# Weight matrices as contiguous chunks, cached keys transposed by the host, and two smaller moves, in a two-layer diffusion trunk

## The chip, the cores and the metric

The kernel runs on one core of a Trainium2 chip. Its metric is the device time of one execution in microseconds (us). Engines are named as in the profile: PE (TensorE), DVE (VectorE), ACT (ScalarE), POOL (GpSimd) and SP (SyncE, which issues most loads). DMA engines move data between HBM and SBUF, the on-chip memory of 128 partitions; PE writes to PSUM, from which ACT and DVE read.

## What is computed

One step of a trunk of two layers, on 128 context tokens and 256 latent tokens, 384 rows of width 2048, all in float32. Each layer modulates its normalized input, projects it, mixes tokens by attention, multiplies by a gate and projects back:

```python
m = silu(cond) @ ada_w + ada_b                       # 2048 -> 3 * 2048, for context and latent
shift, scale, gate = split(m, 3)
h = rmsnorm(x, norm_w) * (1 + scale) + shift
# layer one: 8 heads of differential attention beside a pooling mixer
q, k, v, u, g = split(h @ even_w_in, ...)            # 2048 -> 6144
x = x + gate * ((concat(attn, pool) * silu(g)) @ even_w_out)
# layer two: grouped-query attention, 16 query heads, 4 key heads of 128
q, k, v, g = split(h @ gqa_w_in, ...)                # 2048 -> 5120
x = x + gate * ((attn * silu(g)) @ gqa_w_out)
```

Queries and keys are normalized per head and rotated (latent tokens only). Latent tokens attend to 128 cached context keys as well (`cache_a_k` of layer one, 8 heads of 128 by 128; `cache_c_k` of layer two, 4 heads). Outputs are x of both groups and the new context keys and values.

## The kernel before

All work is traced by the class `Trunk` into a list of items, and `run` goes through it: each item is loaded eight items ahead (`load`), split four items ahead (`split_w`) and then executed. A planner with a model of each instruction's time puts the traced instructions of every engine in order and gives out the buffers; the order in which the code traces them is their priority.

A weight item (`"w"`) is a chunk of 512 KB: two blocks of 128 rows (k blocks) by 512 columns for the token projections (`tok_proj`), or four by 256 for the gates (`gate_proj`); the first chunks of layer one and a few of layer two are single k blocks of 256 KB. `load` fetches it by one DMA on SP's queue into one of two `raw` tiles (L402). `split_w` casts it on ACT into a high part `wh` (L451) and subtracts on DVE for a low part `wl` (L452), three buffers each. Each product is three matmuls of high and low parts (`mm3`, L476 to L478): 128 by 128 by 512 columns for token projections, by 384 for gates. `ada_w` is fetched in loads of 256 KB into `aw` (seven) or `acc` (four) tiles: items `"ada"` go to PE (L413, L544), in groups of one or two blocks of 128 columns at the start (`GROUPS`), items `"adav"` to DVE (L420, L610). A load's row in HBM is a piece of a row of the matrix: 512 bytes for the groups of one block, 1 KB for those of two, 2 KB for 512 columns.

The span begins with X: 12 loads of 256 KB, 48 transposes on PE (L263) whose results ACT copies out (L272), then the modulation in the order of `GROUPS`, each group followed by the chunks of the query and key projections that its rows allow.

Beside the items run generators (`side`, `urgent`), stepped once or twice per weight item: `qk_gen` normalizes, rotates and transposes (L718) a block of 512 query or key columns; `diff_gen` (layer one) and `gqa_gen` (layer two) are the heads; `cache_k` loads four cached heads at a time on POOL's queue into a `kq` tile (L741), transposes them on PE (L745) and, for layer one, ACT copies them into the key tiles `kT` (L752); for layer two they are split into high and low part (`hilo`, L773 and L774).

In layer two `qk_collect` copies the three token tiles of a block of 512 columns out of PSUM into `kq` tiles (L1085; six buffers, which also serve squares, rotation, gates and rows of the modulation), where they stay until L718 has transposed them. `b2` is a pool of 23 tiles of the same size: in layer two it holds the high and low keys and values (16 tiles), the context keys and values (2), the rotary rows, and the transposed probabilities of the heads (L926, L773). `g_finish` takes a gate bank out of PSUM by a tanh on ACT into a `kq` tile (L968) and a product on DVE (L969); the banks are four `mm` tiles, two per pair of gate blocks.

At the end of layer one the output projection runs in four blocks of 512 columns, each over eight chunks and three token tiles. For the last block `HOLD` is 2: `tok_proj` holds the chunk before the last and then runs both of them tile by tile. So the last 36 matmuls are 12 of tile 0, then 12 of tile 1, then 12 of tile 2. When a tile is complete, `out_finish` multiplies by the gate (L1025), adds (L1026), squares (L253), takes the root (L295 to L304) and makes two k blocks of the next h (L325 to L331) for that tile. Then layer two's key and value projections begin, whose first single chunks are split beforehand into `b2` tiles (L442, L443).

Of the kernel before, what the change touches and what calls it, by code (L numbers as in the profile page):

```python
# [17 lines left out]
P = 128  # L18
D = 2048
KT = D // P  # L20
# [31 lines left out]
HOLD = 2  # L52
BAND = 128 + 136 + 136


class Trunk:
# [338 lines left out]
    def load(self, it):  # L395
        nc = self.nc
        if it[0] == "w":
            _, w, kk, c0, nw, _ = it
            nk = len(kk)
            raw = self.p_raw.tile([P, nk, nw], F32, tag="raw", name=f"raw{self.uid()}")  # L400
            src = w[kk[0] * P:(kk[0] + nk) * P, c0:c0 + nw].rearrange("(k p) n -> p k n", p=P)
            self.last_load = nc.sync.dma_start(out=raw, in_=src).ins  # L402
            return raw
        if it[0] == "ada":
# [3 lines left out]
            for kk in range(k0, k0 + self.ada_span(nw), nk):  # L408
# [3 lines left out]
                src = self.io["ada_w"][l, kk * P:(kk + nk) * P, c0:c0 + nw].rearrange("(k p) n -> p k n", p=P)  # L412
                nc.sync.dma_start(out=raw, in_=src)  # L413
                raws += [raw[:, i, :] for i in range(nk)]
            return raws
        if it[0] == "adav":
            _, l, k, c0, nw, _ = it
            nk = 512 // nw
            raw = self.t_aw().rearrange("p (k n) -> p k n", k=nk)
            nc.sync.dma_start(out=raw, in_=self.io["ada_w"][l, k * P:(k + nk) * P, c0:c0 + nw].rearrange(  # L420
                "(k p) n -> p k n", p=P))
            return raw
# [7 lines left out]
        return None  # L430

# [48 lines left out]
    def tok_proj(self, w, c0s, ks, act, finish, hold=1, single=0):  # L480
        banks = {}
        held = []

        def on_chunk(wt, kk, bi):
# [3 lines left out]
            held.append((wt, kk))  # L488
            if kk[0] in ks[-2 * hold:-2]:
                return  # L490
            for t in range(3):
                for (wh, wl), kh in held:
                    for i, k in enumerate(kh):
                        h = act[k]
                        a = (h[:, 0, t * P:(t + 1) * P], h[:, 1, t * P:(t + 1) * P])
                        self.mm3(banks[bi, t], a, (wh[:, i, :], wl[:, i, :]), k == ks[0], k == ks[-1])
                if kk[-1] == ks[-1]:
                    finish(bi, t, banks.pop((bi, t)))
            held.clear()
# [478 lines left out]
    def out_proj(self, l, w, ks, finish):  # L978
# [84 lines left out]
    def build(self):  # L1063
# [9 lines left out]
        W0 = io["even_w_in"][0]  # L1073
        W0o = io["even_w_out"][0]
        W1 = self.w1 = io["gqa_w_in"][0]
        W1o = io["gqa_w_out"][0]
# [68 lines left out]
        main.append(self.call(lambda: self.add_side(self.cache_k(io["cache_a_k"], 8))))  # L1145
# [65 lines left out]
        main.append(self.call(lambda: self.add_side(self.cache_k(io["cache_c_k"], 4, 1))))  # L1211
# [53 lines left out]

_INS = ["x_prompt", "x_sample", "cache_a_k", "cache_a_v", "cache_c_k", "cache_c_v", "c", "c_ctx", "norm_w", "ada_w",
# [24 lines left out]
```

## Time and profile before

| | us |
|---|---|
| median of 3 runs | 1240.4 (1239.6 to 1242.59) |
| the profiled execution | 1239.09 |
| its span | 1237.3 |
| PE busy | 1213.1 (98%) |
| DVE busy | 948.7 (77%) |
| ACT busy | 527.6 (43%) |
| POOL busy | 144.3 (12%) |
| granted TensorE clock, mean | 0.994 |

The span runs from the first to the last instruction; the profiled execution's own time holds a little more than its span. A busy PE is one with a matmul in its pipeline, whose ends are modelled, so neighbouring matmuls overlap in the rows. A timeline row gives start, length, engine, line, operation, tiles written and read, shape and count, and in brackets how long the engine was idle before it and what released it. A granted clock of 1.00 is 2.4 GHz, 0.50 is 1.2 GHz.

### The profile page before, as it was taken

The numbers are of one execution on the slowest core, as the hardware profiler recorded it, in microseconds if no ns is written. First come the engines' busy times: TensorE is split into PE (matmuls) and PEld (weight loads), VectorE is DVE, ScalarE is ACT, GpSimd is POOL, SyncE is SP. The second block draws the span as 40 slices with busy tenths as digits, with TensorE's granted clock in tenths as the row PEclk, the third lists the DMA queues.
The fourth block names the chain that finished last, engine by engine and source line by source line (L and its number), as shares of the span: only waits on it lengthen the run. The fifth ranks groups of instructions, "written<-read, shape, count | busy, mean of one in ns | idle before, by whom it ended". The sixth has DMA issues, their size and how long they took to land.

```text
span 1237.3 us, 18300 instructions
## 1 busy us (share of the span) xinstructions
PE 1213.1 (98%) x6519; PEld 1008.9 (82%) x6519; DVE 948.7 (77%) x1677; ACT 527.6 (43%) x1058; POOL 144.3 (12%) x172
## 2 busy tenths in 40 slices
PE   5999999999999999999999999999999999999998
PEld 4567678777879889997878678888889899998886
DVE  3678569799999799898894699978956985665343
ACT  4323234334445544563334454434544444553221
POOL 0000008611001101001000000423213000000000
PEclk9999999999999999999999999999999999999999
DMA  9999964887777466678785677754633433247652
GB/s 282 331 309 314 338 207 142 258 258 228 253 243 244 136 201 202 184 229 289 236 271 177 198 244 248 226 150 148 191 102 103 148 117 103 86 122 235 188 162 94
DMA packets 174781, 253.50 MB, mean 205 GB/s; under 512 B 14841, under 2 KB 86946, under 8 KB 174690
## 3 DMA queue, kind: packets, MB, share of 16 engines
q1 hardware_dynamic: 169506, 243.57, 62.7%
q0 software_dynamic: 3152, 5.56, 1.4%
q10 hardware_dynamic: 2032, 3.21, 0.7%
q8 instruction: 51, 0.84, 0.3%
q14 instruction: 40, 0.33, 0.1%
HBM read 244.39 MB, written 7.90 MB: 204 GB/s over the span
## 4 chain that ended last, share of the span: by engine, by line
PE 89%; DMA 5%; DVE 3%; ACT 1%; issue 1%; SPq 1%; POOL 0%; DVEq 0%; ACTq 0%; POOLq 0%
PE mm L476 25%; PE mm L477 24%; PE mm L478 24%; PE ax L544 3%; PE ax L476 2%; PE ax L477 2%; PE ax L855 1%; PE ax L478 1%; DVE acc L610 1%; DMA acc<-ada_w 1%; PE ax L875 1%; DMA raw<-even_w_in 1%; PE ax L959 1%; PE ax L924 1%; DMA raw<-even_w_out 1%
## 5 line engine op out<-in xcount | busy, mean ns | idle before, releaser
L451 ACT CAST wh<-raw 128x1024 fp32r<-128x1024 f32 (+1 forms) x242 | 250.8, 1037 | 453.3 <-PE mm L477 160.6
L452 DVE TENSOR_TENSOR wl<-raw,wh 128x1024 fp32r<-128x1024 f32 (+1 forms) x242 | 292.8, 1210 | 172.6 <-ACT wh L451 170.2
L476 PE MATMUL mm<-wh,h 128*128 128x512 f32 x1016 | 400.7, 398 | 2.6 <-ACT h L328 1.2
L477 PE MATMUL mm<-wh,h 128*128 128x512 f32 x1016 | 400.0, 394 | 0.0
L478 PE MATMUL mm<-wl,h 128*128 128x512 f32 x1016 | 392.5, 395 | 0.4 <-DVE wl L452 0.3
L610 DVE SCALAR_TENSOR_TENSOR acc<-aw,sT,acc 128x512 f32<-128x512 f32 x420 | 297.8, 745 | 0.0
L476 PEld LDWEIGHTS mm<-wh,h 128*128 128x128 f32 x1016 | 191.1, 188 | 52.4 <-issue 7.3
L478 PEld LDWEIGHTS mm<-wl,h 128*128 128x128 f32 x1016 | 191.4, 189 | 45.3 <-issue 3.9
L477 PEld LDWEIGHTS mm<-wh,h 128*128 128x128 f32 x1016 | 191.6, 189 | 40.3 <-issue 2.4
L476 PE MATMUL mm<-h,wh 128*128 128x384 f32 x512 | 175.6, 343 | 0.0
L477 PE MATMUL mm<-h,wl 128*128 128x384 f32 x512 | 174.6, 341 | 0.0
L478 PE MATMUL mm<-h,wh 128*128 128x384 f32 x512 | 173.8, 339 | 0.0
L476 PEld LDWEIGHTS mm<-h,wh 128*128 128x128 f32 x512 | 96.6, 189 | 2.6 <-issue 1.8
L477 PEld LDWEIGHTS mm<-h,wl 128*128 128x128 f32 x512 | 96.6, 189 | 2.3 <-issue 1.6
L478 PEld LDWEIGHTS mm<-h,wh 128*128 128x128 f32 x512 | 96.5, 189 | 0.6
L1105 DVE TENSOR_TENSOR b<-mm,b 128x512 f32<-128x512 f32 x72 | 47.8, 684 | 22.6 <-PE mm L478 22.4
L161 POOL TENSOR_TENSOR ss<-ss,mhalf 128x12 f32<-128x12 f32 (+1 forms) x9 | 31.5, 3503 | 263.1 <-DVE ss L159 263.1
L161 POOL TENSOR_TENSOR ti<-ti,mhalf 128x3 f32<-128x3 f32 (+1 forms) x12 | 15.5, 1293 | 211.8 <-DVE ti L159 211.8
L639 POOL DMA_DIRECT2D gates<-kq x32 | 15.7, 495 | 204.2 <-ACT kq L651 141.3
L544 PE MATMUL ax<-aw,sT 128*32 128x256 f32 (+2 forms) x412 | 38.3, 403 | 0.4 <-DMA aw<-ada_w 0.4
L807 ACT ACTIVATE p<-ax,ti 128x384 f32<-128x384 f32 (+1 forms) x48 | 24.2, 508 | 27.1 <-DVE ti L805 26.9
L702 POOL TENSOR_TENSOR kq<-kq,b 128x128 f32<-128x128 f32 x40 | 33.3, 867 | 9.3 <-DVE kq L691 5.9
(208 smaller groups left out, 1240.9 us busy)
## 6 DMA issues: line engine op xcount, KB each, us to landing
aw<-ada_w SPq DMA_DIRECT2D x333, 256.0 KB, 4.0
raw<-even_w_in SPq DMA_DIRECT2D x92, 512.0 KB, 4.6
raw<-gqa_w_in SPq DMA_DIRECT2D x78, 512.0 KB, 3.7
raw<-even_w_out SPq DMA_DIRECT2D x32, 512.0 KB, 4.6
raw<-gqa_w_out SPq DMA_DIRECT2D x32, 512.0 KB, 4.0
acc<-ada_w SPq DMA_DIRECT2D x51, 256.0 KB, 5.9
b<-x_sample SPq DMA_DIRECT2D x16, 256.0 KB, 5.4
kq<-gates SPq DMA_DIRECT2D x16, 256.0 KB, 4.7
```

Source lines behind the costliest of these rows:

```text
L161: nc.gpsimd.tensor_tensor(out=r, in0=t, in1=self.mhalf[:, :n], op=ALU.pow)
L451: nc.scalar.copy(out=wh, in_=raw)
L452: nc.vector.tensor_tensor(out=wl, in0=raw, in1=wh.bitcast(F32), op=ALU.subtract)
L476: mm(out, lhsT=a[0], rhs=b[0], start=start, stop=False, skip_group_check=skip)
L477: mm(out, lhsT=a[1], rhs=b[0], start=False, stop=False, skip_group_check=skip)
L478: mm(out, lhsT=a[0], rhs=b[1], start=False, stop=stop, skip_group_check=skip)
L544: mm = nc.tensor.matmul(b[q:q + 32, half * nw:half * nw + nw], lhsT=self.cond_cols(k0 + i), rhs=raw[i], start=k0 == 0 and i >= span - 4, s ...
L610: nc.vector.scalar_tensor_tensor(out=acc[c], in0=raw[:, i, :], scalar=s, in1=acc[c], op0=ALU.mult, op1=ALU.add)
L639: nc.gpsimd.dma_start(out=self.gates[l, c:c + 1, j * 512 + 256 * i:j * 512 + 256 * i + 256], in_=row[q:q + 1, 0:256])
L702: nc.gpsimd.tensor_tensor(out=t2g[:, :, qq * qd:(qq + 1) * qd], in0=q[:, :, pr * qd:(pr + 1) * qd], in1=sb.broadcast_to([P, G, qd]), op=AL ...
L807: nc.scalar.activation(out=e[:, :n], in_=s, func=AF.Exp, bias=mx[:, i:i + 1], accum_out=sm[:, i:i + 1])
L1105: nc.vector.tensor_tensor(out=r, in0=bank, in1=r, op=ALU.add)
```

## The change

The host cuts `ada_w` and the four large weight matrices into the tiles in which the kernel loads them, and stores each tile as 128 contiguous lines, one per partition: 4 KB a line for the weights (`_tiles`), 2 KB for `ada_w` (`_ada_tiles`). The class `Tiles` finds a chunk in them. Number, order, size and queue of the loads are the same; a chunk of a single k block is half of each line of its tile.

The cached keys come transposed from the host. In layer one each head's keys are loaded straight into the cached columns of its key tile, eight loads of 64 KB on POOL's queue; in layer two they are loaded into a `kq` tile as before and split from there. The transposes and, for layer one, the copies are gone.

The hold at the end of layer one is gone: the last block runs its chunks one by one like the others. And in layer two the three query rows of block 3 are copied into `b2` tiles instead of `kq` tiles.

```diff
+class Tiles:
+    def __init__(self, ap, gates):
+        self.ap, self.gates = ap, gates
+
+    def chunk(self, k, nk, c0, nw):
+        if c0 < self.gates:
+            tile_no = c0 // 512 * 8 + k // 2
+        else:
+            tile_no = self.gates // 512 * 8 + (c0 - self.gates) // 256 * 4 + k // 4
+        t = self.ap[tile_no].rearrange("p (k n) -> p k n", n=nw)
+        return t[:, k % (1024 // nw):k % (1024 // nw) + nk]
...
-            src = w[kk[0] * P:(kk[0] + nk) * P, c0:c0 + nw].rearrange("(k p) n -> p k n", p=P)
+            src = w.chunk(kk[0], nk, c0, nw)
...
-                src = self.io["ada_w"][l, kk * P:(kk + nk) * P, c0:c0 + nw].rearrange("(k p) n -> p k n", p=P)
-                nc.sync.dma_start(out=raw, in_=src)
+                nc.sync.dma_start(out=raw, in_=self.ada_tile(l, c0, kk // nk, nk))
...
+    def ada_tile(self, l, c0, j, nk):
+        return self.io["ada_w"][l * 12 * KT + c0 // P * 4 + j].rearrange("p (k n) -> p k n", k=nk)
...
-            held.append((wt, kk))
-            if kk[0] in ks[-2 * hold:-2]:
-                return
+            wh, wl = wt
             for t in range(3):
-                for (wh, wl), kh in held:
-                    for i, k in enumerate(kh):
...
+            if l == 0:
+                for h in range(b, b + 4):
+                    nc.gpsimd.dma_start(out=self.kT[h][:, P:2 * P], in_=src[h])
+                yield
+                continue
             ck = self.t_kq()
-            nc.gpsimd.dma_start(out=ck.rearrange("p (h d) -> p h d", h=4),
-                                in_=src[0, 0, b:b + 4].rearrange("h t d -> t h d"))
-            pt = self.t_aux()
-            for h in range(4):
-                nc.tensor.transpose(out=pt[:, h * P:(h + 1) * P], in_=ck[:, h * P:(h + 1) * P], identity=self.ident)
+            nc.gpsimd.dma_start(out=ck.rearrange("p (h t) -> p h t", h=4),
+                                in_=src[b:b + 4].rearrange("h d t -> d h t"))
             for h in range(4):
-                src_ = pt[:, h * P:(h + 1) * P]
-                if l:
-                    self.hilo(self.kH[h][:, 0:P], self.kL[h][:, 0:P], src_)
-                    self.kready.add(h)
-                else:
-                    self.evac(1, "c", self.kT[b + h][:, P:2 * P], src_)
+                self.hilo(self.kH[h][:, 0:P], self.kL[h][:, 0:P], ck[:, h * P:(h + 1) * P])
+                self.kready.add(h)
...
-            blk = self.tok_proj(w, [n * 512], ks, yT, lambda bi, t, bank, n=n: finish(n, t, bank),
-                                HOLD if l == 0 and n == 3 else 1)
+            blk = self.tok_proj(w, [n * 512], ks, yT, lambda bi, t, bank, n=n: finish(n, t, bank))
...
-                r = self.t_kq()
+                r = self.t_b2() if l == 1 and blk0 + bi == 3 and not which else self.t_kq()
...
+def _cut(w, nk, nw):
+    n = w.shape[1] // nw
+    return w.reshape(KT // nk, nk, P, n, nw).transpose(3, 0, 2, 1, 4).reshape(-1, P, nk * nw)
+
+
+def _tiles(w, gates):
+    return np.ascontiguousarray(np.concatenate([_cut(w[:, :gates], 2, 512), _cut(w[:, gates:], 4, 256)]))
```

## Rows read from the trace of the kernel before

**Rows 1.** The page: span, busy time of each engine (share of the span) and instructions.

```profile
span 1237.3 us, 18300 instructions
...
PE 1213.1 (98%) x6519; PEld 1008.9 (82%) x6519; DVE 948.7 (77%) x1677; ACT 527.6 (43%) x1058; POOL 144.3 (12%) x172
```

**Rows 2.** The waits of PE, whole span: us in total, times, longest us.

```profile
PE ax L203 <- DMA p<-norm_w: 5.7, 1, 5.7
...
PE ax L476 <- ACT r L773: 2.8, 2, 2.4
PE ax L544 <- DMA acc<-ada_w: 1.8, 3, 1.1
...
PE ax L544 <- DMA aw<-ada_w: 0.4, 1, 0.4
```

**Rows 3.** The table of stretches: busy us of each engine, granted clock, DMA share, GB/s.

```profile
10.00:12.00 2.00, 2.00 (x12) 2.00 (x11) 1.26 (x4) 1.82 (x6) 0.00 (x0) 1.00 1.00 368
15.00:19.00 4.00, 3.80 (x43) 2.97 (x42) 1.01 (x5) 3.43 (x10) 0.88 (x1) 1.00 1.21 297
26.00:32.00 6.00, 5.97 (x27) 4.12 (x28) 1.05 (x3) 0.96 (x2) 0.00 (x0) 0.50 1.15 322
26.00:170.00 144.00, 143.18 (x952) 96.99 (x953) 94.78 (x196) 45.29 (x72) 0.00 (x0) 0.98 0.98 320
694.00:698.00 4.00, 4.00 (x12) 3.13 (x11) 1.23 (x5) 0.56 (x2) 1.33 (x2) 0.57 0.29 95
967.00:971.00 4.00, 3.15 (x12) 3.15 (x13) 4.00 (x9) 1.55 (x5) 0.45 (x1) 0.57 0.73 228
```

**Rows 4.** Timeline of PE, start of the span: start us, us, instruction, idle time before.

```profile
9.19 8.31 PE L263 MATMUL ax<-ident,b 128*128 128x128 f32 x48
...
21.86 0.42 PE L544 MATMUL ax<-acc,sT 128*32 128x128 f32 x8 [1.14 <-DMA acc<-ada_w]
...
26.03 2.07 PE L476 MATMUL mm<-wh,h 128*128 128x512 f32 x4 [1.03 <-ACT h L328]
...
58.03 0.64 PE L544 MATMUL ax<-acc,sT 128*32 128x256 f32 x8 [0.42 <-DMA acc<-ada_w]
```

**Rows 5.** Instructions of single lines: ns min/median/max, first and last start.

```profile
L745 PE MATMUL ax<-ident,kq x12: 272/273/330, 261.1 to 791.3; 128*128 128x128 f32 x12
...
L741 POOL DMA_DIRECT2D kq<-cache_a_k x2: 752/788/825, 249.1 to 250.0; - x2
...
L759 POOL DMA_DIRECT2D b<-cache_a_v x8: 534/542/624, 206.3 to 229.3; - x8
```

**Rows 6.** Timelines of ACT and PE, layer two, block 3 and the first gates.

```profile
920.08 0.58 ACT L1089 COPY kq<-mm 128x512 f32<-128x512 f32 x1
...
964.22 1.01 PE L718 MATMUL ax<-ident,kq 128*128 128x128 f32 x6
...
965.13 0.89 ACT L968 ACTIVATE kq<-mm 128x384 f32<-128x384 f32 x2
...
967.86 0.58 PE L476 MATMUL ax<-r,r 128*128 128x256 f32 x1 [2.38 <-ACT r L773]
...
969.16 0.67 PE L476 MATMUL mm<-h,wh 128*128 128x384 f32 x1
```

**Rows 7.** Timeline of all engines, end of layer one.

```profile
685.01 0.69 DVE L1025 TENSOR_TENSOR kq<-mm,kq 128x512 f32<-128x512 f32 x1 [0.53 <-PE mm L478]
...
686.74 0.69 DVE L443 TENSOR_TENSOR r<-raw,r 128x512 fp32r<-128x512 f32 x1 [1.03 <-ACT r L442]
...
687.34 0.68 DVE L1026 TENSOR_TENSOR b<-b,kq 128x512 f32<-128x512 f32 x1
...
689.57 0.39 PE L476 MATMUL mm<-wh,h 128*128 128x512 f32 x1
...
689.80 0.39 PE L477 MATMUL mm<-wh,h 128*128 128x512 f32 x1
...
692.52 0.47 PE L476 MATMUL mm<-r,h 128*128 128x512 f32 x1
```

More of the change, by code (lines that the diff above doesn't have):

```diff
@@ L51 @@
 EARLY_H = 2
-HOLD = 2
 BAND = 128 + 136 + 136
+class Tiles:
[8 more added lines that the diff above has]
+        return t[:, k % (1024 // nw):k % (1024 // nw) + nk]
 class Trunk:
@@ L419, in load @@
             raw = self.t_aw().rearrange("p (k n) -> p k n", k=nk)
-            nc.sync.dma_start(out=raw, in_=self.io["ada_w"][l, k * P:(k + nk) * P, c0:c0 + nw].rearrange(
-                "(k p) n -> p k n", p=P))
+            nc.sync.dma_start(out=raw, in_=self.ada_tile(l, c0, k // nk, nk))
             return raw
@@ L478, in mm3, with tok_proj @@
         mm(out, lhsT=a[0], rhs=b[1], start=False, stop=stop, skip_group_check=skip)
-    def tok_proj(self, w, c0s, ks, act, finish, hold=1, single=0):
+    def tok_proj(self, w, c0s, ks, act, finish, single=0):
         banks = {}
-        held = []
         def on_chunk(wt, kk, bi):
@@ L487, in on_chunk @@
                     banks[bi, t] = self.t_mm() if bi * 3 + t < 4 else self.t_aux()
-            held.append((wt, kk))
-            if kk[0] in ks[-2 * hold:-2]:
-                return
+            wh, wl = wt
             for t in range(3):
-                for (wh, wl), kh in held:
-                    for i, k in enumerate(kh):
-                        h = act[k]
-                        a = (h[:, 0, t * P:(t + 1) * P], h[:, 1, t * P:(t + 1) * P])
-                        self.mm3(banks[bi, t], a, (wh[:, i, :], wl[:, i, :]), k == ks[0], k == ks[-1])
+                for i, k in enumerate(kk):
+                    h = act[k]
+                    a = (h[:, 0, t * P:(t + 1) * P], h[:, 1, t * P:(t + 1) * P])
+                    self.mm3(banks[bi, t], a, (wh[:, i, :], wl[:, i, :]), k == ks[0], k == ks[-1])
                 if kk[-1] == ks[-1]:
                     finish(bi, t, banks.pop((bi, t)))
-            held.clear()
         return self.w_items(w, c0s, ks, on_chunk, single)
@@ L1071, in build @@
             self.x_transpose(n)
[L1073 to L1076, printed above, removed]
+        W0 = Tiles(io["even_w_in"], 4096)
+        W0o = Tiles(io["even_w_out"], 2048)
+        W1 = self.w1 = Tiles(io["gqa_w_in"], 3072)
+        W1o = Tiles(io["gqa_w_out"], 2048)
         nat = list(range(KT))
@@ L1144, in build @@
         main = []
-        main.append(self.call(lambda: self.add_side(self.cache_k(io["cache_a_k"], 8))))
+        main.append(self.call(lambda: self.add_side(self.cache_k(io["cache_a_kt"], 8))))
         main.append(self.call(lambda: self.new_v(io["cache_a_v"], range(4))))
@@ L1210, in build @@
                 main.append(self.call(lambda: self.rope_tables(1)))
-        main.append(self.call(lambda: self.add_side(self.cache_k(io["cache_c_k"], 4, 1))))
+        main.append(self.call(lambda: self.add_side(self.cache_k(io["cache_c_kt"], 4, 1))))
         for b in range(4):
@@ L1263, in _tables, with _ada_tiles @@
     return {"k_cos_a": ca, "k_sin_a": sa, "k_cos_c": cc, "k_sin_c": sc, "k_band": bands, "k_sel": sel}
+def _cut(w, nk, nw):
[3 more added lines that the diff above has]
+    return np.ascontiguousarray(np.concatenate([_cut(w[:, :gates], 2, 512), _cut(w[:, gates:], 4, 256)]))
+def _ada_tiles(ada_w):
+    tiles = [_cut(ada_w[0, :, part * D + k0 * P:part * D + (k0 + nt) * P], 4 // nt, nt * P)
+             for part in range(2) for k0, nt in GROUPS]
+    tiles += [_cut(ada_w[0, :, 2 * D:], 1, 512), _cut(ada_w[1], 1, 512)]
+    return np.ascontiguousarray(np.concatenate(tiles))
 _INS = ["x_prompt", "x_sample", "cache_a_k", "cache_a_v", "cache_c_k", "cache_c_v", "c", "c_ctx", "norm_w", "ada_w",
@@ L1282 @@
     arrays.update(_tables())
+    arrays["ada_w"] = _ada_tiles(arrays["ada_w"])
+    for name, gates in (("even_w_in", 4096), ("even_w_out", D), ("gqa_w_in", 3072), ("gqa_w_out", D)):
+        arrays[name] = _tiles(arrays[name][0], gates)
+    for name in ("cache_a_k", "cache_c_k"):
+        arrays[name + "t"] = np.ascontiguousarray(arrays.pop(name)[0, 0].transpose(0, 2, 1))
     for name, a in arrays.items():
```

## The prediction, made before the changed kernel ran

> **What bounds the kernel now.** I read the page first [rows 1]: TensorE (PE) is busy 98% of a span of 1237.3 us, so only two things can move the time much: instructions taken off PE, and the 24 us in which PE stands still or runs at the lower clock. The chain of waits is of little use here, since it is nearly all PE. The second view is what PE itself waited for [rows 2]. The list is short: 5.7 us for one row of vectors at the start, 2.8 us for ACT work of layer two, and only 1.8 + 0.4 us for the `ada_w` loads. No wait of PE on a weight load of `even_w_in`, `gqa_w_in` or the output weights appears in that list at all. The third view is the table of stretches [rows 3]. From 26 to 170 us the DMA engines are busy 98% of the time at 320 GB/s, and yet PE is busy 143.18 of 144 us: in that stretch, the one with the most loading, transfers are hidden. The same table shows three places where the granted clock is down: 26 to 32 us (0.50), 694 to 698 (0.57) and 967 to 971 (0.57). All three stand at or right behind a gap of PE; 0.50 is 1.2 GHz of 2.4.
>
> So a better layout of the weights can pay only at the very start, where PE waits for loads with nothing else to do. The other parts of the change touch two of the gaps directly. I make the sum against the profiled execution, which took 1239.1 us (span 1237.3); the median of the runs is 1240.4, so 1.3 us are added at the end. A change under 0.3% (3.7 us) can't be told from none by the measurement.
>
> **Part A, contiguous weights.** Of each chunk the bytes stay the same and the pieces get longer: a first `ada_w` load (four k blocks by 128 columns) goes from 512-byte rows to 2 KB per partition, those of the pairs from 1 KB to 2 KB, a token chunk from two rows of 2 KB to one of 4 KB. The number of loads, their order on SP's queue and their buffers stay. At the start, X is loaded in 2 KB rows and the first loads of `ada_w` come behind it. PE is on the transposes of X from 9.19 to 17.5 us whatever the loads do, then on the eight loads of the first modulation group, the last of which it waits for at 21.86 us, and the first large matmul starts at 26.03 [rows 4]. In the stretch with the 2 KB rows the DMA engines moved 368 GB/s at a share of 1.00, in that with the 512-byte rows 297 GB/s, with a share that reads over 1 [rows 3]. Eight loads of 262,144 bytes are 2.10 MB: 7.1 us at 297 GB/s, 5.7 us at 368. The last lands about 1.4 us sooner, and the first large matmul moves with it, since all between is one chain through ACT and VectorE. The later waits for loads of `ada_w` (0.42 us at 58.03 [rows 4] and about 0.4 more in the sum of [rows 2]) go as well: 2.2 us in all, which is just what PE waited for these loads. The Trainium skill ("DMA: Bandwidth & Descriptors", Specifications) sets the smallest transfer for full rate at 512 bytes; by that page the old rows were long enough and part A would give nothing (+2.2 us on the sum). Here the rows differ, 297 against 368 GB/s [rows 3], and I go by them. Bounds: 0, if the chain from the last load has other limits; and a gain of 5.2, if the whole of the 2.2 goes and the 6 us at clock 0.50 behind it [rows 3], which cost 3.0, go too. For all other loads I count nothing: the work that hides them is PE's own, and without that cover (PE waiting for each landing) they would gain by about a tenth of the transfer. SP's queue gets shorter, never longer.
>
> **Part B, cached keys.** Twelve transposes leave PE [rows 5]. One takes 0.27 us, but they overlap: six transposes of the same shape (L718) take 1.01 us [rows 6], so they start (1.01 - 0.27) / 5 = 0.15 us apart. PE is spared 12 x 0.15 = 1.8 us, and all of this counts because PE is the bound. Eight ACT evacuations of layer one go too; in layer two the split into high and low part stays, read from the loaded tile in place of PSUM. In exchange GpSimd issues eight loads of 64 KB, straight into the key tiles, where there were two of 256 KB: by the 0.54 us of the `cache_a_v` loads, of the same size, 4.3 us in place of 1.6 [rows 5]. Behind them on that queue stand a row of `ada_b` and the four stores of `out_av`, which nothing of PE waits for soon. Between the old loads' issue at 249.1 and the first transpose that read them at 261.1 lie 12 us [rows 5], and the score matmuls come later still, so 2.7 us more are covered. If the cover were gone, PE would wait for at most these 2.7 us. Value: -1.8, bounds -1.8 and +0.9.
>
> **Part C, raw rows.** In layer two the three query rows of block 3 move from the `kq` tiles (six buffers) to the `b2` tiles (23). In the trace of before the last of them is written at 920.08 and the last transposes that read them run at 964.22 [rows 6]: half of the `kq` buffers are tied up for 44 us, while the gate projections run and need one `kq` per bank. And the first gate activations (L968) come only at 965.13, two at once, right behind those transposes and in front of the conversion (L773) that PE waits for 2.38 us; the next gate matmul starts at 969.16 with the clock down [rows 2, 6]. I read it so: all four banks of `mm` are full, no tile is there to empty them, and when one comes free ACT has it all to do at once. With the rows in `b2` the activations can run when their banks are complete. That takes away the 2.38 us, and up to 1.7 us of the stretch at clock 0.57 (4 us with 43% missing) [rows 3]. Together 4.1; I take 3.4, since ACT then still has the same work and the waits may leave a rest. What it costs: of the 23 `b2` tiles the keys, values and rotary rows of layer two hold 19, so the transposed probabilities of the heads (three per head) get one tile where they had four, as long as block 3's rows wait. No row of before shows a wait for `b2`. Nearest row: the 2.38 us that the shortage of `kq` cost. Bounds: -4.1, and the price in the second rival below.
>
> **Part D, the end of layer one.** Before, the last two chunks of the last output block are held back and run token tile by token tile, so tile 0 is complete two tiles of 12 matmuls ahead of the end; after, only the last chunk is, and tile 0 is complete 12 matmuls later than now. Matmuls start 0.23 us apart [rows 7], so that is 2.8 us. The work per tile (gate product, sum, squares, root, scaling, two tiles of h) is one chain of VectorE, ACT, GpSimd and PE. Before it began at 685.01 and the first matmul of layer two started at 692.52 [rows 7]. But in it the sum (L1026) stood from 685.70 to 687.34 behind a weight split (L443) on VectorE, and 2.8 us later that split is long done: 1.6 us come back. On the other hand the three tiles' chains lie closer: tile 1's gate product (0.68 us) falls into tile 0's chain, so I add 0.6. Sum: +2.8 - 1.6 + 0.6 = +1.8. Bounds: 0 (VectorE's order so that tile 0 goes through), and 2.8 + 1.7 = 4.5, if nothing comes back and a second stretch at the lower clock like 694 to 698 follows the longer gap [rows 3].
>
> **Sum.** A -2.2, B -1.8, C -3.4, D +1.8: -5.6 us, 1233.5 in the profiled execution and 1234.8 as median, 0.5% faster. The program is also put in order anew by the planner; I have no row for what that does, and it is inside the widths.
>
> **The rivals.**
> 1. Part C gives nothing, because VectorE and ACT in that stretch are the limit and not the tile: 1234.8 + 3.4 = 1238.2. For it: ACT was busy for all of 967 to 971 [rows 3]. Against it: that the first gate activations wait until the transposes are through.
> 2. Slower: the shortage moves from `kq` to `b2`. Two heads, six tiles, go through one buffer while block 3's rows wait. If a turn costs PE as much as the shortage of `kq` did, 2.4 us, the change is no longer measurably faster from two turns on (+4.8 against -5.6) and is measurably slower from four on; with all six it gives 1234.8 + 14.3 = 1249.1. Against it: gate matmuls fill PE in that stretch.
> 3. The change doesn't do at the start what it says, since the length of the rows doesn't set the rate: the start is as it was, 1234.8 + 2.2 = 1237.0. This is what the page's 512 bytes would come to. Against it: the two rates in [rows 3].
> 4. More than forecast: the shorter gap at the start spares the stretch at half clock (3.0 us) and part D costs nothing (1.8): 1234.8 - 4.8 = 1230.0.
>
> **How the numbers follow.** My forecast has 0.52, rival 1 0.16, rival 2 0.11, rival 3 0.10, rival 4 0.11. The forecast's own range is 1232 to 1238, by the bounds of C and D; its centre lies 1.9 us under the line of 1236.7, so 0.42 of its 0.52 are faster and 0.10 the same. Rival 1 is the same, rival 3 is divided (0.04 faster, 0.06 same), rival 4 is faster, and rival 2 is slower by 0.09 of its 0.11, the rest the same. Faster 0.57, same 0.34, slower 0.09. For 8 in 10 the range goes from 1229.5 (rival 4 inside) to 1242.0, and leaves out most of rival 2.
>
> **What would show it.** A: the first large matmul at about 24.6 us in place of 26.03, and no wait of PE for `ada_w`. B: no transposes at the old line, the first score matmuls not waiting for a DMA. C: gate activations spread between 935 and 965, no gap at 965, full clock there; wrong, if PE or ACT then waits in 920 to 960 for the tiles of the probabilities. D: the first matmul of layer two 1 to 3 us later against the last of layer one; wrong, if the gap is as before. The whole is wrong if PE shows new gaps in 170 to 690 us, where I expect none.

## The result: 1227.95 us, twice the forecast gain

The changed kernel takes 1227.95 us as the median of four runs (1227.69 to 1230.22), the kernel before 1241.3 us beside it on the same chip: a ratio of 0.9896, interval [0.988, 0.9911], or 13.35 us less. I had forecast 1234.8 us, 5.6 us less than before, with a range from 1229.5 to 1242.0. The sign was right, the size was not, and the range was too high at its lower end. Two later comparisons of the same kernel give 0.9903 [0.9886, 0.9921] and 0.9913 [0.9891, 0.9935], so the gain is 10 to 13 us.

The page of the profile after, its span and the busy times (before: [rows 1]); the profiled execution took 1227.69 us.

```profile
span 1225.9 us, 18267 instructions
PE 1205.4 (98%) x6507; PEld 1002.9 (82%) x6507; DVE 946.1 (77%) x1669; ACT 528.3 (43%) x1058; POOL 144.4 (12%) x178
DMA packets 108062, 253.50 MB, mean 207 GB/s; under 512 B 14938, under 2 KB 17411, under 8 KB 107971
```

The packets fall from 174781 to 108062 with the same bytes. PE has 12 instructions fewer (part B) and 7.7 us less busy time. Twelve transposes are 1.8 us of it by step B; the rest is near the 6.8 us that the three stretches of half clock, 13.6 us long in all, cost before. The table of stretches is that of [rows 3], with two stretches moved to where the same work now lies; the column before the last two is the granted clock, the last one GB/s.

```profile
10.00:12.00 2.00, 2.00 (x11) 2.00 (x10) 1.14 (x4) 1.84 (x6) 0.00 (x0) 1.00 1.06 398
15.00:19.00 4.00, 4.00 (x47) 2.98 (x49) 1.02 (x5) 3.27 (x10) 1.59 (x2) 1.00 1.06 398
26.00:32.00 6.00, 5.38 (x48) 3.29 (x47) 1.91 (x3) 2.18 (x4) 0.00 (x0) 1.00 1.05 386
26.00:170.00 144.00, 142.94 (x953) 97.17 (x952) 98.15 (x205) 47.42 (x76) 0.00 (x0) 1.00 0.91 317
684.00:692.00 8.00, 6.71 (x34) 4.62 (x35) 7.08 (x23) 6.04 (x16) 1.90 (x3) 1.00 0.43 117
958.00:968.00 10.00, 10.00 (x64) 9.97 (x63) 10.00 (x18) 3.68 (x7) 0.00 (x0) 1.00 0.67 198
```

From 15 to 19 us the loads move 398 GB/s where they moved 297 [rows 3]; the engines' share in 26 to 170 us falls from 0.98 to 0.91 at about the same GB/s. And in this profile the clock is 1.00 in all three places where it was down before (0.50, 0.57, 0.57). The 1.00 of the first stretch is no reading, here or in [rows 3]: the records of the clock begin at 14.8 us here and at 15.0 before. Ahead of them the transposes of X start 0.213 us apart, behind them 0.109, in both profiles, so PE began at the lower level, and the change does not touch that.

The timeline of PE at the start (before: [rows 4]):

```profile
19.90 0.48 PE L552 MATMUL ax<-aw,sT 128*32 128x128 f32 x6
21.11 0.44 PE L576 MATMUL ax<-ident,kq 128*128 128x128 f32 x2 [0.73 <-ACT kq L559]
...
23.40 0.91 PE L489 MATMUL mm<-wh,h 128*128 128x512 f32 x2 [0.89 <-ACT h L340]
```

The first large matmul starts 2.63 us sooner than in [rows 4]; I had said 1.4. The start scatters between executions of one kernel (26.03 and 26.80 us in two profiles of the kernel before; 23.40, 23.77 and 23.56 in three of the changed one), but the two groups lie well apart. The wait of 1.14 us for the last load is gone, those for ACT (0.73 and 0.89) are left. Call a matmul large if it is the first of a `mm3` and has 384 or 512 columns; there are 1600. The n-th of one trace can be set against the n-th of the other: the lead is 2.63 us at the first, 4.8 at 180 us, 7.0 at 540, 8.9 at 735, 10.3 at 905 and 11.4 at the end. About 5 us of it arise in the first 180 us, where I had 2.2.

The end of layer one on PE (before: [rows 7]), and the raw rows and gate activations of layer two (before: [rows 6]):

```profile
682.05 0.39 PE L491 MATMUL mm<-wl,h 128*128 128x512 f32 x1
683.97 0.46 PE L314 MATMUL ax<-p,ones 128*128 128x128 f32 x2 [1.53 <-DVE ti L307]
685.72 0.46 PE L314 MATMUL ax<-p,ones 128*128 128x128 f32 x2 [1.29 <-DVE ti L307]
685.93 0.48 PE L489 MATMUL mm<-r,h 128*128 128x512 f32 x1
```

```profile
946.86 0.88 ACT L974 ACTIVATE kq<-mm 128x384 f32<-128x384 f32 x2
...
956.01 0.49 ACT L974 ACTIVATE kq<-mm 128x384 f32<-128x384 f32 x1 [1.02 <-PE mm L491]
...
959.79 0.48 ACT L974 ACTIVATE kq<-mm 128x384 f32<-128x384 f32 x1
```

From the last matmul of layer one to the first of layer two it is 3.88 us (682.05 to 685.93), where it was 2.49 (690.03 to 692.52): step D, as forecast. The first two gate activations still run back to back, but at 946.86, while the transposes of block 3 (940.6 to 950.4) are going on; the next come one at a time, and no gap of PE follows the transposes.

### The profile page after: what moved, and what is told of

Same layout as the page of the kernel before. It is cut to its first block, busy times and chain, and to the rows that moved or that the text cites. A ratio compares the mean times of both kernels' runs of the same rounds, so it can differ in the third digit from the quotient of the medians.

```text
span 1225.9 us, 18267 instructions
## 1 busy us (share of the span) xinstructions
PE 1205.4 (98%) x6507; PEld 1002.9 (82%) x6507; DVE 946.1 (77%) x1669; ACT 528.3 (43%) x1058; POOL 144.4 (12%) x178
## 2 busy tenths in 40 slices
DMA packets 108062, 253.50 MB, mean 207 GB/s; under 512 B 14938, under 2 KB 17411, under 8 KB 107971
## 4 chain that ended last, share of the span: by engine, by line
PE 90%; DMA 4%; DVE 3%; issue 1%; ACT 1%; SPq 0%; POOL 0%; ACTq 0%; DVEq 0%; POOLq 0%
PE mm L489 25%; PE mm L491 25%; PE mm L490 25%; PE ax L552 3%; PE ax L489 2%; PE ax L490 2%; PE ax L491 1%; PE ax L861 1%; DMA raw<-even_w_in 1%; DMA aw<-ada_w 1%; DVE acc L618 1%; DMA raw<-even_w_out 1%; PE ax L881 1%; PE ax L726 1%; PE ax L965 1%
## 5 line engine op out<-in xcount | busy, mean ns | idle before, releaser
L813 ACT ACTIVATE p<-ax,ti 128x384 f32<-128x384 f32 (+1 forms) x48 | 24.3, 508 | 24.8 <-DVE ti L811 24.5
L779 ACT CAST r<-ax 128x256 fp32r<-128x256 f32 (+1 forms) x60 | 21.0, 361 | 30.9 <-PE ax L930 28.7
```

The costliest lines, as they stand in the source:

```text
L779: self.nc.scalar.copy(out=hi, in_=src)
L813: nc.scalar.activation(out=e[:, :n], in_=s, func=AF.Exp, bias=mx[:, i:i + 1], accum_out=sm[:, i:i + 1])
```

## Experiments

Each ratio is to the kernel before on the same chip. The clock is the mean granted clock over all executions of the kernel; a fall of 0.001 is 1.2 us, and one execution's clock is given to 0.001. (1 - clock) x span is the time lost to the lower clock, clock x span what is left at full clock; I use both as means over the executions only. Half clock that sets in behind PE's last matmul is in these means too, where nothing is lost by it: up to 1.2 us (in the profile of e14 all of its 0.001). With that and the scatter of the executions a difference of two such means is good to between 1 and 2 us.

| run | edit | median us | ratio, interval | clock |
|---|---|---|---|---|
| e0 | kernel before | 1239.17 | 0.9994 [0.9983, 1.0005] | 0.9957 |
| e1 | A alone | 1231.64 | 0.9932 [0.9913, 0.9952] | 0.9990 |
| e2 | after without C | 1229.66 | 0.9920 [0.9904, 0.9936] | 0.9968 |
| e3 | after without D | 1231.00 | 0.9928 [0.9909, 0.9947] | 0.9982 |
| e4 | after | 1229.00 | 0.9903 [0.9886, 0.9921] | 0.9975 |
| e5 | after without B | 1230.52 | 0.9917 [0.9896, 0.9938] | 0.9980 |
| e6 | A, `ada_w` only | 1233.23 | 0.9940 [0.9923, 0.9956] | 0.9990 |
| e7 | A, other weights only | 1238.44 | 0.9977 [0.9963, 0.9992] | 0.9956 |
| e8 | e6 with short rows | 1239.57 | 1.0011 [0.9998, 1.0025] | 0.9951 |
| e9 | before, 18 fillers | 1244.81 | 1.0048 [1.0026, 1.0070] | 0.9966 |
| e10 | after, 22 fillers | 1232.48 | 0.9955 [0.9939, 0.9971] | 0.9988 |
| e11 | after without A | 1233.89 | 0.9964 [0.9947, 0.9980] | 0.9952 |
| e12 | before, 6 fillers | 1240.64 | 1.0004 [0.9990, 1.0019] | 0.9968 |
| e13 | after, 4 fillers | 1229.63 | 0.9910 [0.9888, 0.9932] | 0.9970 |
| e14 | after | 1229.61 | 0.9913 [0.9891, 0.9935] | 0.9975 |

The kernel before had clocks of 0.9957, 0.9946, 0.9958 and 0.9960 on the four chips of e0 to e3, e4 to e7, e8 to e11 and e12 to e14 (13, 13, 22 and 13 executions).

**e0, the kernel before again.**

> The kernel before, unchanged, to see whether its three stretches at the lower clock (26 to 32, 694 to 698, 967 to 971 us; mean granted clock 0.994) belong to the program or to the run. Theory 'gaps': every run has them, clock 0.994 to 0.995 in each, ratio 1.000. Rival 'chance': some runs show a clock of 0.998 or more and are 3 to 7 us shorter.

1239.17 us. Its profile has half clock at 26.1 to 32.9, 695.1 to 698.5 and 971.6 to 975.0 us, the same three places as [rows 3]. Over its ten executions the granted clock lies between 0.994 and 0.997 and never at 1.0: about 5.3 us lost, in every execution some. Over all 61 executions of the kernel before it lies between 0.991 and 0.999.

**e1, the layout of all weights alone** (keys, raw rows and hold as before).

> The kernel before with part A alone (contiguous chunks of ada_w and of the four weight matrices); hold, raw rows and cached keys as before. Theory 'most of the gain is the start': first large matmul at about 23.4 us in place of 26.0 (-2.6) and no stretch at half clock behind it (-3.4), some more in the loading stretch: -6 to -8 us. Rival 'sum as forecast': -2.2 us. The stretches at 694 and 967 stay, as nothing there is changed.

8.2 us under the kernel before, where step A had 2.2. The first large matmul starts at 22.93. The lead over the kernel before is 5.5 us at 180 us, hardly grows until 540 (5.8) and is 7.5 at the end. At full clock (clock x span) e1 is 4.3 us under its kernel before, 1228.1 against 1232.5, and the lower clock costs 1.2 us in place of 5.3. So by these means about half of A's gain is work and waits and half is half clock that is not drawn. I had expected the stretches at 694 and 967 us to stay. Its profile has the first (686.8 to 690.2 us) and not the second, though PE's wait of 2.4 us in front of that place is as before.

**e6 and e7, the two halves of the layout.** In e6 only `ada_w` is a contiguous chunk, in e7 only the projection weights (shown against e1, shortened):

```
e6: -            src = w.chunk(kk[0], nk, c0, nw)
    +            src = w[kk[0] * P:(kk[0] + nk) * P, c0:c0 + nw].rearrange("(k p) n -> p k n", p=P)
e7: -    nc.sync.dma_start(out=raw, in_=self.ada_tile(l, c0, kk // nk, nk))
    +    nc.sync.dma_start(out=raw, in_=self.io["ada_w"][l, kk * P:(kk + nk) * P, c0:c0 + nw].rearrange(...))
```

> The kernel before with nothing but the ada weights laid out as chunks; the other weights, keys, raw rows and the hold as before. Theory (the start is paced by the ada loads, which are the only loads there): the first large matmul 2.6 to 3.1 us sooner, as in the run with all weights laid out, and a median 3 to 6 us under the kernel before, the larger end if the stretches of half clock at the start and at the end of layer one go as well. Rival (the gain of the layout is the sum of many small ones all along the weights): the first large matmul sooner, but less than 3 us in the median.

> The kernel before with nothing but the four projection weights laid out as chunks; the ada weights, keys, raw rows and the hold as before. Theory (start and ada loads carry the layout's gain; later loads are hidden, with some 0.8 us of waits to give back): within 0 to 2 us under the kernel before, first large matmul at 26 us as before. Rival (the layout gains all along): 4 us or more under the kernel before, with the gap to it growing steadily from 70 us to the end.

e6 gains 6.9 us, a little more than expected; e7 1.7 us by the medians (1.0 to 4.6 by the interval), as expected. The parts add up: 6.9 + 1.7 = 8.6 against 8.2 in e1. In e6 the lead is 2.67 us at the first large matmul and 4.95 at 180 us, then it stands at 5.3 until 540. By the means over its executions 1.7 us of e6's gain are at full clock and 5.4 us are the clock. e7's first large matmul starts at 27.51 us, later than the 26 I expected; X, whose loads the edit leaves alone, has landed only at 16.12 us in that execution (14.12 in the kernel before). The first stretches of e6 and of e7:

```profile
15.00:19.00 4.00, 3.56 (x40) 2.46 (x38) 1.01 (x5) 3.69 (x11) 0.89 (x1) 1.00 1.06 400
26.00:32.00 6.00, 5.42 (x48) 3.30 (x47) 1.88 (x3) 2.18 (x4) 0.00 (x0) 1.00 1.05 386
```

```profile
15.00:19.00 4.00, 3.85 (x40) 3.16 (x42) 1.64 (x7) 4.00 (x12) 0.88 (x1) 1.00 1.18 310
26.00:32.00 6.00, 5.47 (x40) 3.45 (x40) 2.17 (x6) 1.54 (x4) 0.00 (x0) 0.50 1.14 299
```

With the `ada_w` chunks the loads run at 400 GB/s and the clock is at 2.4 GHz behind the start; without them it is 310 GB/s and 1.2 GHz.

**e8, contiguous chunks with short rows.** As e6, but inside the chunk the k blocks follow each other, so each partition reads rows of 512 bytes (1 KB for the pairs; the lines are shortened):

```
-    transpose(3, 0, 2, 1, 4).reshape(-1, P, nk * nw)
+    transpose(3, 0, 1, 2, 4).reshape(-1, P, nk * nw)
-    ada_w[tile].rearrange("p (k n) -> p k n", k=nk)
+    ada_w[tile].rearrange("p n -> (p n)").rearrange("(k p n) -> p k n", k=nk, p=P)
```

> The run with only the ada weights laid out anew, with one thing changed: each chunk is still one contiguous piece of 256 KB in memory, but inside it the k blocks follow each other, so that each partition reads rows of 512 bytes (1 KB for pairs) as in the kernel before. Theory (the length of the rows sets the rate of the loads): the start is as before, first large matmul at 25.5 to 26.5 us, about 300 GB/s from 15 to 19 us, a stretch of half clock at the start, and a median within 2 us of the kernel before. Rival (it is the contiguous place in memory that counts): the first large matmul at 23 to 23.5 us, about 398 GB/s, and 6 to 8 us under the kernel before.

```profile
15.00:19.00 4.00, 3.64 (x42) 2.68 (x41) 1.72 (x7) 4.00 (x12) 0.88 (x1) 1.00 1.19 300
26.00:32.00 6.00, 5.41 (x29) 3.63 (x27) 1.35 (x3) 1.58 (x4) 0.00 (x0) 0.54 1.11 305
```

Nothing is left of the gain: 1.0011 [0.9998, 1.0025], 300 GB/s, the first large matmul at 26.64, half clock behind it. The same bytes from the same contiguous 256 KB, only in shorter rows, are as slow as the old layout. So in these loads the length of the rows sets the rate, and not the place in memory; the third rival is out. The Trainium skill ("DMA: Bandwidth & Descriptors", Specifications) gives 512 bytes as the least for full rate; here, from 15 to 19 us, 512-byte rows had 294 to 310 GB/s in seven profiles and 2 KB rows 393 to 403 in ten, so the measurement decides against the page.

**e11, all but the layout** (parts B, C and D on the old weights).

> The changed kernel with the layout of all weights undone, that is the kernel before with the keys, the raw rows and the end of layer one changed (parts B, C and D). If the parts add up (the whole was 11 to 13 us, the layout alone 8): 3 to 5 us under the kernel before, with the first large matmul at 26 us and the half clock behind it back. By my sum for these parts (-1.8, -3.4, +1.8): 3.4 us under it. If the layout is needed for the rest to pay (the planner's order is another): within 1.5 us of the kernel before.

5.0 us under the kernel before by the medians (2.5 to 6.6 by the interval). At full clock it is 4.8 us under it (1227.0 against 1231.8), and the lower clock costs as much as before, 5.9 against 5.2 us. The parts add up to 8.2 + 5.0 = 13.2 us; the whole was 13.35 in the first comparison and 11.1 and 10.0 in the two later ones (e4, e14), all within the intervals. By these means the clock is A's part alone. As expected, e11's profile has the late start (26.34 us) and the half clock behind it (25.0 to 31.8 us) back.

**e5, the keys undone.** In the changed kernel `cache_k` loads by token and transposes on PE again.

> The changed kernel with the cached keys loaded token by token and transposed on TensorE again, as before. Theory (step B, 12 transposes of 0.15 us on an engine that is the bound): 1.8 us more than the changed kernel of this chip, 1229 to 1231 us, with no wait of a score matmul for a key's load in either. Rival (the 512-byte pieces of the stacked keys or the transposes' places cost something else, up to the bound +0.9): the same as the changed kernel or up to 0.9 us less.

1230.52 against 1229.00 in e4: 1.5 us. Set against the changed kernel's trace, e5's large matmuls go from 0.15 us ahead at the first to 1.67 behind at the end, and the clock is 1.00 in both profiles: 1.8 us, the size of step B. The medians alone would not carry it: the two intervals overlap. Nor is it shown that the transposes are all of it: in the kernel before, those of one group start 0.11 us apart, so 12 of them take 1.3 to 1.4 us.

**e2, the raw rows undone.**

```
-    r = self.t_b2() if l == 1 and blk0 + bi == 3 and not which else self.t_kq()
+    r = self.t_kq()
```

> The changed kernel with part C undone (block 3's rows in kq tiles again). Theory: the wait of PE for the conversion behind the gate activations comes back (2.4 us, and 1.7 us of lower clock): +2.4 to +4.1 us. Rival 'the wait went for another reason, such as a new order': under +1 us and no gap near 955.

The waits of PE in e2 and, in the second fence, in the changed kernel:

```profile
PE ax L489 <- ACT r L779: 2.4, 1, 2.4
```

```profile
PE ax L489 <- ACT r L779: 0.5, 1, 0.5
```

Where these waits end, in e2 and in the changed kernel:

```profile
959.01 0.39 PE L489 MATMUL ax<-r,r 128*128 128x256 f32 x1 [2.37 <-ACT r L779]
```

```profile
919.48 0.39 PE L489 MATMUL ax<-r,r 128*128 128x256 f32 x1 [0.46 <-ACT r L779]
```

The wait that step C named is back, and in e2's profile half clock follows it (960.0 to 963.4 us). The changed kernel's 0.46 us is another wait, at 919.48, ahead of the transposes; the one that step C named is gone there altogether. But the whole is only 0.9 to 3.0 us slower than the changed kernel (ratio 0.9920 against its 0.9896 to 0.9913), not 3.4, and the intervals overlap, so the times alone do not show a gain of C. In the two profiles, from the 1001st large matmul to the last, e2 takes 413.16 us and the changed kernel 411.81: 1.35 us more, which is less than the 1.7 us that the half clock alone costs e2 there. So the 1.9 us of wait by which the two fences differ come back in other places. PE's order is another in e2 from 909 us on; which places take the 1.9 us is open.

**e3, the hold put back.**

```
-    blk = self.tok_proj(w, [n * 512], ks, yT, lambda bi, t, bank, n=n: finish(n, t, bank))
+    blk = self.tok_proj(..., HOLD if l == 0 and n == 3 else 1)
```

(Shortened; the loop of `tok_proj` that holds the chunks is back too.)

> The changed kernel with part D undone (the hold of two chunks at the end of layer one is back). By the forecast's step D: -1.8 us. Theory from the two traces (from the last matmul of layer one to the first of layer two 3.9 us after against 2.5 before): -1.4 us. Rival 'the planner's order decides': 0 to +2 us.

By step D this should have been 1.8 us faster than the changed kernel. It is 1.9 to 4.0 us slower by the ratios (0.9928 against 0.9896 to 0.9913), with intervals that overlap a little: a loss is likely and not shown, but the gain of 1.8 us is not there. At the place itself the step holds: from the last matmul of layer one to the first of layer two it is 2.20 us with the hold (683.63 to 685.83), 3.88 without. But the order of PE's instructions is another from 687 us on, and in 800 to 850 us e3 has waits that the changed kernel has not:

```profile
PE ax L732 <- DVE kq L721: 1.7, 1, 1.7
PE ax L490 <- ACT r L785: 0.7, 1, 0.7
```

From the 1001st large matmul to the last e3 takes 415.27 us, 3.46 more than the changed kernel. It loses there more than the hold gains. I read that as the order that the planner made from this program, not as a price of the hold as such; no run changes the order alone. For it: in e1, with the hold and without C, these waits are smaller: from 809 to 839 us the lead of the changed kernel over e1 grows by 0.8 us, over e3 by 3.4.

**e4 and e14, the changed kernel again.**

> The changed kernel again, on the chip of the next three runs, as their control. If the gain is in the code and in which stretches of half clock it draws: a median of 1227 to 1229 us, a ratio of 0.988 to 0.992, and at most one stretch of half clock in the profiled execution (there was none). If the missing stretches of half clock were luck of the one profile and of that chip: two or three stretches of 3.4 us here, and a median of 1230 us or more.

> The changed kernel on the chip of the two runs beside it, as their control: 1227.5 to 1229.5 us, a ratio of 0.988 to 0.992, and a mean granted clock of 0.996 to 1.0 that differs between executions of the same program.

The gain holds in three comparisons. But e4's profile, where I had allowed one stretch at most, has half clock at 24.5 to 27.9 and 686.7 to 690.1 us, where the first profile and that of e14 have none, with PE's instructions in the same order in e4 as in the first profile, and waits of about the same length. The stretch from 684 to 692 us in e4 (in the first profile it read 1.00):

```profile
684.00:692.00 8.00, 6.56 (x27) 4.17 (x28) 6.21 (x23) 4.98 (x13) 1.90 (x3) 0.79 0.26 92
```

Over the twelve executions of the changed kernel the clock is 0.998, so 2.5 us are lost to it on average, against 5.5 over the 61 of the kernel before. At full clock the means are 1224.7 and 1232.3 us. So of 10.6 us in these means some 7.6 are work and waits and some 3.0 the clock.

**e9, e10, e12 and e13, fillers in PE's waits.** To see whether PE's standing still draws the half clock, transposes of the identity, whose results nobody reads, were put into its waits, pinned behind the instruction before (shortened):

```
+    def fill(self, n):
+        d = self.t_mm()
+        for _ in range(n):
+            self.tc.keep_in_program_order(
+                self.nc.tensor.transpose(out=d[:, 0:P], in_=self.ident, identity=self.ident))
e9, e10: 6, 6, 6 and 3, 5, 6 of them: ahead of the last ada tile, behind it, behind the transposes of mod(0)
e12: the first 6 of e9 alone      e10: 8, e13: 4 more behind rstd_tiles(0, 1) at the end of layer one
```

> The kernel before with 18 transposes of the identity put into PE's waits at the start (6 in the wait for the last ada load, 6 in that for the copy on ACT, 6 in that for the first tile of h); nobody reads their results. Theory (the half clock behind the start is drawn by PE standing still there): the clock is 1.00 from 26 to 33 us where it was 0.50 in both profiles of before, the first large matmul at 26.0 to 26.6 us, and the median 2.4 to 3.4 us under the kernel before. Rival (the half clock comes from something else, such as the amount of work that sets in): the stretch stays, and the median is 0 to 1 us above the kernel before.

> The changed kernel with the same kind of fillers: 3, 5 and 6 transposes in PE's waits at the start and 8 in the second wait at the end of layer one (the first wait there, 1.5 us, stays). Theory (as in the run beside it): no stretch of half clock at the start in any profile, fewer at the end of layer one, a mean granted clock of 0.999 to 1.0 in all executions, and a median of 1226 to 1227.5 us, 1 to 2 us under the changed kernel. Rival (fillers only cost): 1228.5 to 1230 us.

> The kernel before with 6 transposes of the identity in PE's one wait for the last ada load (1.1 us, at 21 us); the order of all other work is as before on every engine, which was not so in the runs with fillers at three places. The two waits behind it, 1.0 us each, stay. Theory (half clock follows where PE has stood still long enough, so a shorter rest spares it or shortens it): half clock behind the start for 0 to 3.4 us in place of 6.8, and 1 to 3.4 us under the kernel before, with no cost elsewhere. Rival (the two waits that stay are enough to draw it): 6.8 us of half clock as before, and a median within 0.5 us of the kernel before.

> The changed kernel with 4 transposes of the identity in the second of its two waits at the end of layer one (1.3 us), the order of all other work unchanged. Theory (as beside it): no stretch of half clock at 687 us, a mean granted clock 0.0005 to 0.0015 higher than that of the changed kernel beside it, and a median 0 to 1.5 us under it. Rival (chance decides whether the clock falls there): clock and median within 0.5 us of it.

The stretch behind the start in e9 and, in the second fence, in e12; below it the waits of PE in e9 from 20 to 130 us:

```profile
26.00:32.00 6.00, 5.55 (x51) 3.43 (x55) 1.81 (x4) 2.10 (x5) 0.00 (x0) 1.00 0.95 269
```

```profile
26.00:32.00 6.00, 4.79 (x26) 3.13 (x27) 1.72 (x4) 1.91 (x4) 0.00 (x0) 0.72 1.17 304
```

```profile
PE mm L476 <- ACT wh L451: 7.1, 4, 3.8
PE mm L476 <- ACT h L328: 0.8, 1, 0.8
```

With fillers in the waits, the old layout has full clock behind the start (e9: 1.00 where [rows 3] has 0.50), though its loads run at the old 294 GB/s from 15 to 19 us. The waits from the last `ada_w` load to the first large matmul, 3.6 us in the kernel before, are 1.3 us there (the last, 0.85, is hardly shorter). With one wait filled there are 3.4 us of half clock in place of 6.8 (e12), and another 3.4 at 61.7 us. So in these two profiles the half clock at the start goes with PE's standing still and not with the rate of the loads, which supports that the layout works through it. They are one profile each, and in e9 the order of PE's work is another too, so it is not proof. As a remedy the fillers failed: in e9 and e10 the planner put the splits of the weights elsewhere, PE waited 7.1 and 4.0 us for them, and a new stretch of half clock stood behind, at 101 and at 95 us. e9 is 5.9 us slower than the kernel before beside it, e10 by the ratios 5 to 7 us slower than the changed kernel. In e12 and e13, where the order of all else is unchanged, no gain can be measured. e13's profile has its half clock at 686.3 to 689.7 us all the same. The four transposes take only 0.2 us off the two waits there (2.6 us in place of 2.8), and the changed kernel without them has it or has it not, so this profile decides nothing.

No version beat the changed kernel.

## Why the prediction was wrong, point by point

**What bounds the kernel.** Right that only PE's instructions and its idle or slow time count, and that transfers from 26 to 170 us are hidden. But the 24 us that I gave for idle and slow time (1237.3 less 1213.1) are idle time alone. The three stretches of half clock lie inside PE's busy time and cost another 6.8 us. I then priced one of them in the sum, where C touched the gap, and that at the start only as a bound. That was the root of the error.

**Part A: the failed step.** The sentence that failed is "a better layout of the weights can pay only at the very start, where PE waits for loads": the place was right for most of it, but the price was only the wait, and the slow matmuls behind the wait were left out of the sum. I had the clock's 3.0 us at the start as a bound and as part of rival 4, with a chance of 0.11. (The stretch is 6.8 us long and costs 3.4; my window of 26 to 32 us cut it.) It came, by halves: all five profiles of kernels with 512-byte rows and no fillers at the start have 6.8 us of half clock behind the start, the nine with the chunks have 0 in five, 3.4 in three and 6.8 in one. By the means the clock gives 4.1 us in e1 and 5.4 in e6, where the sum had nothing.

The term of the first loads was too small as well. I took 7.1 and 5.7 us for the eight loads; from the landing of X's last they took 7.7 us before and 5.4 after (7.1 to 7.7 in the seven profiles with short rows, 5.3 to 6.1 in the ten with chunks). My 368 GB/s came from two microseconds of X's loads, which are alike in all kernels and read 252 to 398 GB/s there; the chunks ran at 398. The first large matmul starts 2.63 us sooner (3.10 in e1, 2.67 in e6), not 1.4. Of the 0.8 us that I added for later waits, the 0.4 for an `aw` tile stand at 24.36 us, ahead of the first large matmul, and so were counted twice. The other weights gave 1.7 us (e7), where I counted nothing; which of their loads gain is not settled. Their landing is a little sooner, as I said (a load of `even_w_in` takes 4.2 us in place of 4.6). At full clock A is 4.3 us in e1, and 1.7 and 1.4 for its halves in e6 and e7, against my 2.2. So what the sum clearly lacked is the clock.

**Part B: right, in part by luck.** 1.8 us forecast, 1.5 by the medians and 1.8 by the traces (e5). No PE wait for a key's load appeared in the changed kernel; in e1 and e6, where the old transposes follow the faster start, they wait 0.5 and 1.0 us for the keys of layer two, which part B spares as well. But I took the 0.15 us of a transpose from L718, and the twelve themselves start 0.11 us apart, so something else makes up the rest. And the eight copies of layer one that go were on VectorE (L270; DVE has 8 instructions fewer, ACT as many as before), not on ACT; neither bounds that stretch.

**Part C: the mechanism right, the size not shown to be.** The 2.38 us of [rows 2] are gone, and the activations are spread as said (946.86, 956.01, 959.79). No wait for `b2` came, so rival 2 is out: PE's one wait from 900 to 960 us, the 0.46 at 919.48, has its like in the kernel before (0.46 at 843.68). Of the forecast 3.4 us the ratios show 0.9 to 3.0, not clear of the noise, and in the one pair of profiles nothing but the half clock is left of them.

**Part D: right at its place; for the whole its sign is not borne out.** The gap grew by 1.4 us (2.49 to 3.88; forecast 1.8, bounds 0 to 4.5). The half clock that I feared behind the longer gap follows it in four of eight profiles without the hold (e2, e4, e11, e13), and the shorter gap in seven of nine with it, so the 1.4 us did not decide it. And e3 is slower with the hold by 1.9 to 4.0 us (not clear of the noise), since PE's waits in 800 to 850 us came out worse in that program; that the planner's order is the cause is my reading. I had put the planner "inside the widths"; here it moves as much as each of the parts.

**The sum.** B, C and D together: 3.4 us forecast, 5.0 measured (e11), its interval reaching from 2.5 to 6.6. A: 2.2 forecast, 8.2 measured (e1). Rival 4 at 1230.0 was nearest, and the range ended half a microsecond under it, as if it were a floor. But its two terms can come together with a better rate at the start: 1230.0 less the 1.2 us by which the first large matmul came sooner than said is 1228.8.

**What would show it.** No new gap came between 170 us and the end of layer one, the first large matmul came sooner than I said, and PE has one wait of 0.3 us left for `ada_w`. The gate activations are spread and followed by no gap, as said for C.

## What to carry to other kernels

Price a stretch of half clock as part of the wait in front of it: where loads at a start come in short rows, what they cost is the wait and the slow matmuls that can follow it, here 2.6 and up to 3.4 us. Count half clock by the share of profiles that have it, since the same gap has it in one execution and not in the next. Lay out what is loaded while nothing else can run so that each partition reads one long row; the rest of the weights, hidden behind matmuls, gained 1.7 of 1240 us. In a kernel that a planner orders, the order of all that follows can change with an edit, and what the edit is worth at its place (the hold: 1.4 us) need not be left at the end, so measure it both ways.

## What was not expected of the hardware

**The clock differs between executions of one program.** The changed kernel's granted clock lies between 0.996 and 1.0 in its twelve executions, and half clock stands in one of its three profiles at two places where the others have none, with the same instructions and waits of about the same length. The wait that part C removes stands in nine profiles, and half clock follows it in five; in the eight without it there is none at that place. The Trainium skill ("TensorE: Matmul & The Clock Gate", What's actually happening) says that how many matmuls run slow at a kernel's start varies from run to run of one kernel; the traces agree, as 11, 24 and 27 of the 48 transposes of X run at the slower pace in the three profiles of the changed kernel. That it also varies behind waits in the middle is shown by the stretch at 686.7 us alone, which e4 has and the other two have not. A single profile is therefore no measure of what the clock costs, its mean over executions is.

**Row length and rate.** Loads of 256 KB to 128 partitions moved 294 to 310 GB/s in rows of 512 bytes and 393 to 403 in rows of 2 KB (15 to 19 us, seven and ten profiles), and 300 against 400 in chunks that are contiguous in memory either way (e8, e6).
